# Reciprocal roots by one polynomial of degree 4, and low parts of twelve weight tiles by an adding DMA

## The chip, the cores and the metric

The kernel runs on one core of a Trainium2 chip. The time is that of the device for one execution, in microseconds, and a comparison of two kernels is one of medians on the same chip. TensorE (PE in the profile) multiplies matrices, VectorE (DVE), ScalarE (ACT) and GpSimd (POOL) work on tiles of 128 partitions, and SyncE (SP) issues DMAs. Each engine takes its own instructions in order, and semaphores make them wait for each other.

## What is computed

One step of a two-layer streaming encoder over 1,088 rows (1,024 of a new stream, 64 of a running one) of width 1,024, all in fp32. Layer 0 is a state-space mixer with a SwiGLU FFN, layer 1 a band attention with a SwiGLU FFN; each part stands between two root-mean-square norms.

```python
def rmsnorm(x, w):
    xf = x.astype(jnp.float32)
    y = xf * lax.rsqrt(jnp.mean(xf * xf, axis=-1, keepdims=True) + EPS)
    return (y * w.astype(jnp.float32)).astype(x.dtype)

def swiglu(u, w_in, w_out):
    g, up = jnp.split(u @ w_in, 2, axis=-1)
    return (jax.nn.silu(g) * up) @ w_out
...
        xp = xp + rmsnorm(mp, nw[1])
        xs = xs + rmsnorm(ms, nw[1])
        xp = xp + rmsnorm(swiglu(rmsnorm(xp, nw[2]), ffn_w_in[layer], ffn_w_out[layer]), nw[3])
        xs = xs + rmsnorm(swiglu(rmsnorm(xs, nw[2]), ffn_w_in[layer], ffn_w_out[layer]), nw[3])
```

`D_MODEL` is 1024 and the hidden width of the FFN 2816, so `w_in` is 1024 x 5632: 44 weight tiles of 128 columns, 22 for the gate and 22 for the other half.

## The kernel before

**Products of split numbers.** TensorE multiplies in a shortened format, fp32r. Each operand is split into a high part, its value rounded to fp32r, and a low part, the remainder; a product is three matmuls: high by high, high by low, low by high (lines 403 to 405, 1225 to 1227 and 1395 to 1397).

**Weight tiles.** The class `Weights` handles every weight tile in the order of use. `load` has SyncE fetch a tile of 128 x 1024 numbers, 512 KB, into one of two `raw` buffers (L220). `part` then writes the two parts into one slot of a ring: ScalarE copies the tile into fp32r, which gives the high part `h` (L300), and VectorE subtracts `h` from the tile, which gives the low part `lo` (L301). Some calls name GpSimd for the subtraction. After that the raw buffer is free for the next load, and SyncE, which takes its DMAs in order, waits in `load` until it is. The ring `hl` has three slots; while an FFN begins there are two more, `hx`.

**The start of an FFN.** `back` runs the last projection of the mixer or the attention (`project`), and while that runs, side tasks work on its results: `chain` applies the norm after the mixer, adds the residual, and applies the norm before the FFN for one quarter of the rows; `op_build` forms sums of blocks of the result and splits them into high and low parts (L1087, L1099, L1100). `ffn_plan` lists the weight tiles of the FFN: first ten single tiles, two for each of the first `NB0 = 5` hidden tiles, which `plain_pairs` multiplies in the plain way for the first 512 rows, then pairs of tiles for `run_pair`, which saves an eighth of the matmuls by sums of blocks. The ten single tiles are loaded and split while the projection and the norms still run.

**Reciprocal roots.** A norm sums squares: ScalarE squares a block (L425, L428) and GpSimd adds it to `ssum` (L429), through two buffers for squares. Then `rstd` has TensorE sum over partitions (`nst`, L436), and VectorE computes the reciprocal root on a column or so per block of 128 rows: mean plus epsilon (L442), a first guess from the bits of the number (L443), and two rounds of four instructions (L446 to L453), each a step of third order. `diag` puts the result on a diagonal (L457, tile `dg`), `bcast` spreads it over the partitions by a matmul with the constant matrix `frac` (tile `nbp`, L465), which carries a factor that the last round leaves out, and ScalarE copies that to `rb` (L469). `rstd` is called 40 times.

**Order.** The order of TensorE's instructions is written out: a main stream of matmul units, and side tasks that it starts when their time has come by its own count of microseconds, so an `nst` or `nbp` matmul stands at a fixed place among the units, and TensorE waits there if its input is late. The order on the other engines is set by a scheduler before the run, by priorities and expected times; `HIP`, `CHP` and `OPP` are such priorities. Steps of the roots have a high one.

Of the kernel before, what the change touches and what calls it, by code (L numbers as in the profile page):

```python
# [11 lines left out]
AF = mybir.ActivationFunctionType  # L12
ALU = mybir.AluOpType
# [20 lines left out]
FT = 22  # L34
# [26 lines left out]

PGS = (0,), (1,), (2,), (3,), (4,)
NB0 = 5
BIG = 1e30
MMR = 2360.0

C_NW = 0
# [129 lines left out]
class Weights:  # L197
# [95 lines left out]
    def part(self, it, key, ring, v, eng=None):  # L293
        if ring is not self.half:
            ring = self.hl if ring or self.hl.free() else self.hx
            self.used.append(ring)
        t, n = ring.get(), v.shape[1]
        h, lo = t[:, 0, :n], t[:, 1, :n]
        with self.tc.high_priority(self.pri):
            self.nc.scalar.copy(h, v)  # L300
            (eng or self.eng or self.nc.vector).tensor_tensor(lo, v, h, op=ALU.subtract)  # L301
        it[key] = h, lo
# [20 lines left out]
def hybrid_kernel(  # L323
# [5 lines left out]
    V, A, G, PE = nc.vector, nc.scalar, nc.gpsimd, nc.tensor  # L329
# [16 lines left out]
    ones = cp.tile([P, P], F32, name="ones")  # L346
    G.memset(ones, 1.0)
    frac = cp.tile([P, P], F32, name="frac")
    G.memset(frac, 9.0 / 64.0)
    pcs = cp.tile([P, NPC], F32, name="pcs")  # L350
    A.activation(ones[:, 0:1], ones[:, 0:1], AF.Square)

# [1 line left out]
    for _ in range(17):  # L354
# [13 lines left out]
    W = Weights(  # L368
        nc, Ring(wp, "raw", RAWB, [P, 1024]), Ring(wp, "hl", HLB, [P, 2, 1024], F32R),
        Ring(None, "half", 0, [P, 2, 512], F32R), Ring(None, "tt", 0, [P, 1024]),  # L370
    )
# [13 lines left out]
    def ax(name):  # L385
        return pax.tile([P, 512], F32, tag="ax", name=name)
# [8 lines left out]
    def passes(ps, w, rhs, ks, n, parts=2, first=True, last=True):  # L395
# [4 lines left out]
        for i, (kw, k) in enumerate(ks):  # L400
# [4 lines left out]
            PE.matmul(ps[:, :n], l_, xh, start=False, stop=(last and i == nk - 1))  # L405
            st.t += 3 * n / MMR
            if (i + 1) % cut == 0 and i + 1 < nk:
# [23 lines left out]
    def rstd(ssum, inv, r, nb, more=None):  # L431

        sp, ts = ax("nst"), [ssum] if more is None else [ssum, more]
        for i in range(nb):
            for j, t in enumerate(ts):
                PE.matmul(  # L436
                    sp[:, i:i + 1], t[:, i * P:(i + 1) * P], ones[:, 0:1], start=(j == 0), stop=(j == len(ts) - 1)
                )
        with tc.high_priority(HIP):
            v = nsb.tile([P, 12], F32, tag="nv", bufs=2, name="nv")  # L440
            a, h, y = v[:, 0:nb], v[:, 4:4 + nb], v[:, 8:8 + nb]
            V.tensor_scalar(a, sp[:, :nb], inv, EPS, op0=ALU.mult, op1=ALU.add)  # L442
            V.tensor_scalar(y.bitcast(I32), a.bitcast(I32), -0.5, float(0x5F3759DF), op0=ALU.mult, op1=ALU.add)  # L443

            for it in range(2):
                V.tensor_tensor(h, y, y, op=ALU.mult)  # L446
                if it:
                    V.scalar_tensor_tensor(a, h, 9.0 / 64.0, a, op0=ALU.mult, op1=ALU.mult)
                    V.scalar_tensor_tensor(h, a, -10.0 / 3.0, a, op0=ALU.add, op1=ALU.mult)
                else:  # L450
                    V.tensor_tensor(h, h, a, op=ALU.mult)
                    V.scalar_tensor_tensor(h, h, -10.0 / 3.0, h, op0=ALU.add, op1=ALU.mult)
                V.scalar_tensor_tensor(r if it else y, h, 5.0, y, op0=ALU.add, op1=ALU.mult)  # L453

    def diag(r3, nb):
        dg = DG.get()
# [15 lines left out]
    def rb_steps(ssum, n, out, wait=None, rb=None, more=None):  # L472

        nb = (n + P - 1) // P
        nr = nsb.tile([P, 4], F32, tag="nr", bufs=2, name="nr")
        rstd(ssum, 1.0 / D, nr[:, :nb], nb, more)
        yield 0.2, 0, DG.free
        with tc.high_priority(HIP):
            dg = diag(nr[:, :nb], nb)
        yield 0.1, wait or RB_WAIT  # L480
        with tc.high_priority(HIP):
            out.append(bcast(dg, 0, n, rb))
        yield 0.5, 0
# [107 lines left out]
    with ExitStack() as es:  # L591
# [8 lines left out]
        mask = sb1.tile([P, P], F32, name="mask")  # L600
        G.memset(mask, BIG)
        G.affine_select(mask, mask, pattern=[[1, P]], compare_op=ALU.is_ge, fill=-BIG, base=0, channel_multiplier=-1)
        stk = sb1.tile([64, 32], F32, name="stk")
# [167 lines left out]
        def ssd_task(j, s):  # L771
# [112 lines left out]
            if jj == 3:  # L884
                yield 0, 5.0
                rstd(ssg[:, s * 384:(s + 1) * 384], 1.0 / 512, rst[:, 3 * s:3 * s + 3, g], 3)
                rst_done.add((g, s))
                yield 0.3, 0
# [283 lines left out]

    def ffn_plan(layer):
        w1, w2 = w_f1[layer], w_f2[layer]
        W.plan(*[dict(src=[w1[i]]) for t_ in range(NB0) for i in (t_, FT + t_)])
        for t_ in [*range(NB0, FT), *range(NB0)]:
            W.plan(dict(src=[w1[t_], w1[FT + t_]]))
        for s in range(NSL):
            for m in range(KD):
                for k0, nk in KCH:  # L1180
                    W.plan(dict(src=[w2[m][:, k0 * P:(k0 + nk) * P]], n=nk * P))
# [27 lines left out]
    def run_pair(t_, pr, bs, ends, ops, hd, px, tmp, apart=False):  # L1209
# [3 lines left out]
        for (p_, key, c0, i), b in [(x, b) for b in bs for x in PRODS] if apart else [(x, b) for x in PRODS for b in bs]:  # L1213
# [9 lines left out]
            for k in range(4):  # L1223
# [4 lines left out]
                if k == 1:  # L1228
                    st.run(6 * n / MMR)
            st.t += 6 * n / MMR  # L1230
            if b in ends:
# [34 lines left out]
    def back(layer, start, cpost, xsrc, xmid, cpre, cpost2, xout, rb_out, done2):  # L1266
# [3 lines left out]
        with ExitStack() as es:  # L1270
# [79 lines left out]
            with ExitStack() as e2:  # L1350
# [18 lines left out]
                for r in ops[0].rings["a21"]:  # L1369
                    r.put()  # L1370
                for t_, bs, ends in [(t_, (0, 1), (0,) if t_ == FT - 1 else ()) for t_ in range(NB0, FT)] + [(t_, (1,), (1,) if t_ == NB0 - 1 else ()) for t_ in range(NB0)]:
                    run_pair(t_, W.get(), bs, ends, ops, hd, px, tmp, t_ == NB0)
                    W.pri = 0
# [7 lines left out]
            for s, (o, n) in enumerate(SL):  # L1381
# [3 lines left out]
                for m in range(KD):  # L1385
                    ps = px.tile([P, 512], F32, tag="mm", name="po")
                    for k0, nk in KCH:
                        w = W.get()
                        h, v = w["w"]
                        for k in range(k0, k0 + nk):  # L1390
# [7 lines left out]
                            if m == KD - 1:  # L1398
                                for c_ in c:
                                    cells.put(c_)  # L1400
                            st.run(3 * n / MMR)
                        W.put()
# [18 lines left out]
    def start_ssd(ops, px, after, dn):  # L1421
# [10 lines left out]
        st.spawn(op_build(ops[1], dn))  # L1432

    ffn_plan(0)
    rbp = pool(ctx, "rbp", side="right")
    rba = [rbp.tile([P, 384], F32, tag=f"rbf{s}", name="rbf") for s in range(NSL)]
# [4 lines left out]

    NEG = -BIG
    H2 = slice(0, 64), slice(64, 128)
# [7 lines left out]
    for b in range(2):  # L1451
        W.plan(*[dict(src=[w_o[m]]) for mg in MGS for m in mg])
    ffn_plan(1)
    done = done2
    uo = {}
# [403 lines left out]
```

## Time and profile before

| | |
|---|---|
| median of three runs | 3099.95 us (3099.75 to 3102.89) |
| the profiled execution | 3100.79 us, with a span of 3099.1 us in the trace |
| mean granted clock of TensorE | 0.988 |
| VectorE's subtractions in L301 | 407 instructions, of which 20 write `hx` |
| ScalarE's busy share | 45% |
| GpSimd's busy share | 28% |
| HBM over the span | 103 GB/s |

In the rows of a timeline the columns are: start, duration, engine, line, operation, the tile written and the tiles read, the shape, and how many were merged; in brackets the idle time of that engine before, and what ended it. Rows with a line of code and `x40` group instructions, with the shortest, median and longest duration in nanoseconds. A row of the windows gives a stretch of time and the busy time of each engine in it.

### The profile page before, as it was taken

How to read it: one execution, taken by the hardware profiler on the slowest of the kernel's cores; microseconds unless marked ns; L12 is line 12 of the kernel's file. 1: busy time of each engine (PE TensorE's matmuls, PEld its weight loads, DVE VectorE, ACT ScalarE, POOL GpSimd, SP SyncE). 2: the span in 40 equal slices, each digit the busy share in tenths (PEclk: the TensorE clock that was granted, in tenths of full speed). 3: DMA queues.
4: the chain of work that ended last, by engine and by line, in shares of the span. 5: the costliest groups of instructions: out<-in, count | busy, mean ns of one | idle time of the engine just before them, and what ended most of it. 6: DMA issues, size and time to landing. Idle time of an engine off the chain costs nothing.

```text
span 3099.1 us, 56834 instructions
## 1 busy us (share of the span) xinstructions
PE 2996.7 (97%) x21761; PEld 2913.0 (94%) x21761; DVE 2138.0 (69%) x4671; ACT 1407.2 (45%) x2500; POOL 875.6 (28%) x999
## 2 busy tenths in 40 slices
PE   8999999999999999999999999999998999999998
PEld 7899999999999999999999888889898999999997
DVE  7878788786778455584666888877778645575544
ACT  6656565664443222344443554444543322244432
POOL 2333333331334433441233111100053334342112
PEclk9999999999999999999999999999999999999999
DMA  3011111124534222245664121112344222245654
GB/s 118 32 59 48 59 51 59 49 79 150 167 119 122 78 74 80 90 146 169 201 193 127 61 68 61 54 60 61 122 137 142 80 77 75 79 123 177 207 183 131
DMA packets 174784, 322.85 MB, mean 104 GB/s; under 512 B 17168, under 2 KB 124560, under 8 KB 174512
## 3 DMA queue, kind: packets, MB, share of 16 engines
q1 hardware_dynamic: 174448, 319.16, 33.3%
q8 instruction: 171, 2.80, 0.4%
q14 instruction: 101, 0.83, 0.1%
q0 software_dynamic: 64, 0.07, 0.0%
HBM read 256.56 MB, written 62.60 MB: 103 GB/s over the span
## 4 chain that ended last, share of the span: by engine, by line
PE 77%; DVE 12%; DMA 4%; issue 3%; ACT 3%; POOL 2%; SPq 0%; DVEq 0%; POOLq 0%; ACTq 0%
PE mm L403 8%; PE px L1225 7%; PE px L1226 7%; PE px L1227 7%; PE mm L405 7%; PE mm L404 7%; PE po L1397 5%; PE po L1395 5%; PE po L1396 5%; PE mmx L403 2%; PE mmx L404 2%; PE mmx L405 2%; PE po L1651 2%; DVE hl L301 2%; PE ptp L1628 2%
## 5 line engine op out<-in xcount | busy, mean ns | idle before, releaser
L301 DVE TENSOR_TENSOR hl<-raw,hl 128x1024 fp32r<-128x1024 f32 (+1 forms) x299 | 369.5, 1237 | 316.0 <-ACT hl L300 315.7
L403 PE MATMUL mm<-r,hl 128*128 128x384 f32 (+2 forms) x1664 | 561.1, 337 | 7.4 <-ACT BT L737 5.9
L405 PE MATMUL mm<-r,hl 128*128 128x384 f32 (+2 forms) x1664 | 540.7, 325 | 0.6 <-DVE hl L301 0.6
L404 PE MATMUL mm<-r,hl 128*128 128x384 f32 (+2 forms) x1664 | 540.4, 325 | 0.0
L300 ACT CAST hl<-raw 128x1024 fp32r<-128x1024 f32 (+1 forms) x302 | 305.2, 1014 | 304.6 <-PE po L1397 96.5
L1226 PE MATMUL px<-r,hl 128*128 128x288 f32 (+1 forms) x1192 | 349.8, 293 | 0.0
L403 PEld LDWEIGHTS mm<-r,hl 128*128 128x128 f32 x1664 | 316.9, 190 | 16.6 <-issue 6.8
L429 POOL TENSOR_TENSOR ssum<-ssum,sq 128x256 f32<-128x256 f32 (+3 forms) x153 | 170.1, 1114 | 546.9 <-ACT sq L428 543.6
L1225 PE MATMUL px<-r,hl 128*128 128x288 f32 x1056 | 311.5, 295 | 6.5 <-DVE u L1240 6.5
L404 PEld LDWEIGHTS mm<-r,hl 128*128 128x128 f32 x1664 | 317.1, 191 | 0.6 <-DVE r L552 0.2
L405 PEld LDWEIGHTS mm<-r,hl 128*128 128x128 f32 x1664 | 316.2, 190 | 1.0 <-DVE hl L301 1.0
L1227 PE MATMUL px<-r,hl 128*128 128x288 f32 x1056 | 310.8, 294 | 0.0
L1227 PE MATMUL px<-rx,hl 128*128 128x256 f32 x816 | 228.9, 281 | 7.3 <-DVE hl L301 7.3
L1225 PE MATMUL px<-rx,hl 128*128 128x256 f32 x816 | 229.8, 282 | 0.0
L1226 PEld LDWEIGHTS px<-r,hl 128*128 128x128 f32 x1192 | 223.8, 188 | 0.1
L1396 PE MATMUL po<-rx,hl 128*128 128x384 f32 (+1 forms) x640 | 207.5, 324 | 0.0
L1225 PEld LDWEIGHTS px<-r,hl 128*128 128x128 f32 x1056 | 198.5, 188 | 8.2 <-DVE u L1240 8.2
L1395 PE MATMUL po<-rx,hl 128*128 128x384 f32 (+1 forms) x608 | 199.3, 328 | 0.0
L1397 PE MATMUL po<-rx,hl 128*128 128x384 f32 (+1 forms) x608 | 197.6, 325 | 0.9 <-DVE hl L301 0.9
L1227 PEld LDWEIGHTS px<-r,hl 128*128 128x128 f32 x1056 | 198.3, 188 | 0.0
L1226 PE MATMUL px<-rx,hl 128*128 128x256 f32 x680 | 190.7, 280 | 0.0
L258 POOL TENSOR_TENSOR tt<-raw 128x512 f32<-128x512 f32 x44 | 60.2, 1367 | 400.0 <-DMA raw<-in_w_f_dram 278.6
(343 smaller groups left out, 8135.5 us busy)
## 6 DMA issues: line engine op xcount, KB each, us to landing
raw<-in_w_f_dram SPq DMA_DIRECT2D x204, 512.0 KB, 3.7
raw<-in_w_in_dram SPq DMA_DIRECT2D x40, 512.0 KB, 3.6
raw<-in_w_f_dram SPq DMA_DIRECT2D x48, 384.0 KB, 3.2
sg<-hscr SPq DMA_DIRECT2D x88, 192.0 KB, 3.7
raw<-in_w_so_dram SPq DMA_DIRECT2D x32, 512.0 KB, 3.9
raw<-in_w_kv_dram SPq DMA_DIRECT2D x18, 512.0 KB, 3.6
raw<-in_w_o_dram SPq DMA_DIRECT2D x16, 512.0 KB, 3.8
sg<-hscr SPq DMA_DIRECT2D x44, 160.0 KB, 3.7
```

The lines of the kernel that those rows point to most:

```text
L300: self.nc.scalar.copy(h, v)
L301: (eng or self.eng or self.nc.vector).tensor_tensor(lo, v, h, op=ALU.subtract)
L403: PE.matmul(ps[:, :n], h_, xh, start=(first and i == 0), stop=False)
L404: PE.matmul(ps[:, :n], h_, xl, start=False, stop=False)
L405: PE.matmul(ps[:, :n], l_, xh, start=False, stop=(last and i == nk - 1))
L429: (eng or G).tensor_tensor(ssum[:, :n], ssum[:, :n], q[:, :n], op=ALU.add)
L1225: PE.matmul(ps, wh, ah[:, k, :], start=(k == 0), stop=False)
L1226: PE.matmul(ps, wh, al[:, k, :], start=False, stop=False)
L1227: PE.matmul(ps, wl, ah[:, k, :], start=False, stop=(k == 3))
L1395: PE.matmul(ps[:, :n], wh, xh, start=(k == 0), stop=False)
L1396: PE.matmul(ps[:, :n], wh, xl, start=False, stop=False)
L1397: PE.matmul(ps[:, :n], wl, xh, start=False, stop=(k == FT - 1))
```

## The change

It has two parts.

First, `rstd`. In place of two rounds of four instructions there is one polynomial: with y the first guess and h = a y y, a near 1, VectorE evaluates a polynomial of degree 4 in h by nested products and multiplies it by y. Two of the ten instructions of a root fall away. The leading factor of the polynomial is left out there and put into the constant matrix `frac`, as the factor before it was.

Second, `part`. For the first six single tiles of each FFN (`NACC = 3` hidden tiles, two tiles each) ScalarE writes the high part as before and then its negative into the slot of the low part. GpSimd issues a DMA that reads the tile from HBM once more and adds it to that: the low part. VectorE's subtraction for these twelve tiles falls away; the DMA stands in GpSimd's queue and waits there for the negation. The raw buffer is needed only for the copy.

```diff
@@ -61,7 +61,11 @@
 NB0 = 5
+
+NACC = 3
 BIG = 1e30
+
+RL, RP = 0.274060676, (-5.145514965, 10.804858208, -11.997578621, 8.987062454)
@@ -296,6 +300,14 @@
         h, lo = t[:, 0, :n], t[:, 1, :n]
+        if it.get("acc"):
+
+            with self.tc.high_priority(self.pri):
+                self.nc.scalar.copy(h, v)
+                self.nc.scalar.activation(lo, h, AF.Copy, scale=-1.0)
+            self.nc.gpsimd.dma_start(lo, it["src"][0], accum_op=ALU.add)
+            it[key] = h, lo
+            return
         with self.tc.high_priority(self.pri):
             self.nc.scalar.copy(h, v)
@@ -346,7 +358,7 @@
-    G.memset(frac, 9.0 / 64.0)
+    G.memset(frac, RL)
@@ -442,15 +454,13 @@
-            for it in range(2):
-                V.tensor_tensor(h, y, y, op=ALU.mult)
-                if it:
-                    V.scalar_tensor_tensor(a, h, 9.0 / 64.0, a, op0=ALU.mult, op1=ALU.mult)
-                    V.scalar_tensor_tensor(h, a, -10.0 / 3.0, a, op0=ALU.add, op1=ALU.mult)
-                else:
-                    V.tensor_tensor(h, h, a, op=ALU.mult)
-                    V.scalar_tensor_tensor(h, h, -10.0 / 3.0, h, op0=ALU.add, op1=ALU.mult)
-                V.scalar_tensor_tensor(r if it else y, h, 5.0, y, op0=ALU.add, op1=ALU.mult)
+
+            V.tensor_tensor(h, y, y, op=ALU.mult)
+            V.tensor_tensor(h, h, a, op=ALU.mult)
+            V.scalar_tensor_tensor(a, h, RP[0], h, op0=ALU.add, op1=ALU.mult)
+            V.scalar_tensor_tensor(a, a, RP[1], h, op0=ALU.add, op1=ALU.mult)
+            V.scalar_tensor_tensor(a, a, RP[2], h, op0=ALU.add, op1=ALU.mult)
+            V.scalar_tensor_tensor(r, a, RP[3], y, op0=ALU.add, op1=ALU.mult)
@@ -1172,7 +1182,7 @@
-        W.plan(*[dict(src=[w1[i]]) for t_ in range(NB0) for i in (t_, FT + t_)])
+        W.plan(*[dict(src=[w1[i]], acc=t_ < NACC) for t_ in range(NB0) for i in (t_, FT + t_)])
```

## The prediction

> **What bounds the kernel now.** I read the page first, then TensorE's timeline for its gaps, then the other engines' timelines around the largest of them.
>
> ```profile
> span 3099.1 us, 56834 instructions
> PE 2996.7 (97%) x21761; PEld 2913.0 (94%) x21761; DVE 2138.0 (69%) x4671; ACT 1407.2 (45%) x2500; POOL 875.6 (28%) x999
> L301 DVE TENSOR_TENSOR hl<-raw,hl 128x1024 fp32r<-128x1024 f32 (+1 forms) x299 | 369.5, 1237 | 316.0 <-ACT hl L300 315.7
> ```
>
> TensorE is busy for 97%, and the change removes none of its matmuls. Work taken from another engine pays only where TensorE waits for that engine: about 100 us in all. TensorE's waits at the start of the second layer's FFN, and others that stand behind a reciprocal root:
>
> ```profile
> 43.66 1.42 PE L465 MATMUL nbp<-dg,frac 128*128 128x384 f32 x4 [0.39 <-DVE dg L457]
> 969.49 0.58 PE L1227 MATMUL px<-rx,hl 128*128 128x256 f32 x1 [4.10 <-DVE hl L301]
> 1691.51 2.29 PE L436 MATMUL nst<-ones,ssum 128*128 128x1 f32 x10 [2.61 <-DVE ssum L1342]
> 2304.62 0.70 PE L465 MATMUL nbp<-dg,frac 128*128 128x256 f32 x2 [2.30 <-DVE dg L457]
> 2316.28 0.67 PE L465 MATMUL nbp<-dg,frac 128*128 128x256 f32 x2 [4.01 <-DVE dg L457]
> 2341.97 1.30 PE L465 MATMUL nbp<-dg,frac 128*128 128x288 f32 x2 [5.39 <-DVE nr L453]
> 2399.23 0.38 PE L1227 MATMUL px<-rx,hl 128*128 128x256 f32 x1 [3.18 <-DVE hl L301]
> ```
>
> Between 2296 and 2342 TensorE loses 2.30 + 4.01 + 5.39 = 11.7 us to three broadcasts of reciprocal roots. The windows say which engine is full there (columns: PE, PEld, DVE, ACT, POOL, granted clock, DMA share, GB/s):
>
> ```profile
> 2290.00:2310.00 20.00, 17.70 (x133) 17.18 (x132) 14.98 (x25) 10.76 (x26) 16.94 (x19) 1.00 0.56 173
> 2310.00:2330.00 20.00, 15.99 (x115) 15.73 (x114) 19.44 (x32) 13.18 (x22) 7.03 (x8) 0.91 0.37 123
> 2330.00:2350.00 20.00, 14.23 (x104) 13.52 (x102) 18.71 (x42) 7.80 (x13) 4.45 (x6) 0.91 0.29 89
> 885.00:915.00 30.00, 30.00 (x239) 29.89 (x238) 14.36 (x31) 10.72 (x17) 8.93 (x9) 1.00 0.41 136
> ```
>
> From 2310 to 2342 it is VectorE; before that, 2296 to 2310, GpSimd with 16.94 of 20. The last row is the same work in the first layer: VectorE half idle, TensorE full. The two FFN starts must be priced apart.
>
> **The low parts, second layer.** Six of VectorE's subtractions (L301) go; these are the six:
>
> ```profile
> 2301.94 1.76 DVE L301 TENSOR_TENSOR hl<-raw,hl 128x1024 fp32r<-128x1024 f32 x1
> 2306.60 1.23 DVE L301 TENSOR_TENSOR hl<-raw,hl 128x1024 fp32r<-128x1024 f32 x1 [2.03 <-ACT hl L300]
> 2310.52 0.80 DVE L1170 SCALAR_TENSOR_TENSOR rx<-rx,pcs,rb 128x256 f32<-128x256 f32 x1 [1.81 <-ACT rb L469]
> 2316.06 1.21 DVE L301 TENSOR_TENSOR hx<-raw,hx 128x1024 fp32r<-128x1024 f32 x1
> 2324.42 1.22 DVE L301 TENSOR_TENSOR hx<-raw,hx 128x1024 fp32r<-128x1024 f32 x1
> 2332.47 1.21 DVE L301 TENSOR_TENSOR hl<-raw,hl 128x1024 fp32r<-128x1024 f32 x1
> 2338.08 1.22 DVE L301 TENSOR_TENSOR hl<-raw,hl 128x1024 fp32r<-128x1024 f32 x1
> 2341.74 0.15 DVE L453 SCALAR_TENSOR_TENSOR nr<-nv 128x3 f32<-128x3 f32 x1
> ```
>
> From 2310.52, where VectorE gets the broadcast root, to 2341.74 it runs without a gap worth a microsecond, and the wait that ends at 2341.97 ends with it. Four of the six lie inside: 1.21 + 1.22 + 1.21 + 1.22 = 4.86 us. The first two lie before an idle of 1.81 us, so what they free is lost in that wait. Inside the stretch the shorter polynomial also drops 6 small instructions (2 from each of three roots), at 0.07 to 0.2 us of pitch as they lie interleaved: 0.4 to 1.2, taken as 0.6. Gain: **-5.5 us**, if the stretch starts when it did.
>
> It will not quite. What VectorE waited for at 2310.5 is a copy on ScalarE, which is queued behind squares that alternate with GpSimd's sums:
>
> ```profile
> 2297.60 1.05 ACT L300 CAST hl<-raw 128x1024 fp32r<-128x1024 f32 x1
> 2298.59 8.08 POOL L429 TENSOR_TENSOR ssum<-ssum,sq 128x256 f32<-128x256 f32 x9
> 2301.01 0.42 ACT L428 ACTIVATE sq<-rx 128x256 f32<-128x256 f32 x1 [0.40 <-DVE nv L446]
> 2305.53 1.03 ACT L300 CAST hl<-raw 128x1024 fp32r<-128x1024 f32 x1
> 2307.05 4.00 POOL L429 TENSOR_TENSOR ssum<-ssum,sq 128x288 f32<-128x288 f32 x4 [0.38 <-ACT sq L428]
> 2310.05 0.38 ACT L469 COPY rb<-nbp 128x256 f32<-128x256 f32 x1
> ```
>
> Two of the new negations fall here, behind the casts at 2297.60 and 2305.53. I price one like the cast, 1.05 us; ScalarE's gap between squares is 0.40, so each pushes the next square by 0.65. GpSimd, without a gap in 2298.6 to 2306.7, gets two DMA issues, and those wait in its in-order queue for the negations; behind them stand the sums, and for those wait the squares, the root's copy and TensorE. The trace has two DMAs issued by GpSimd, of 32 and 36 KB, both plain:
>
> ```profile
> L612 POOL DMA_DIRECT2D pbs<-in_pb_dram x1: 705/705/705, 2.5 to 2.5; - x1
> DMA to landing us min/median/max: 5.5/5.5/5.5
> L614 POOL DMA_DIRECT2D scs<-in_sconv_dram x1: 540/540/540, 3.2 to 3.2; - x1
> 869.27 2.29 POOL L429 TENSOR_TENSOR ssum<-ssum,sq 128x288 f32<-128x288 f32 x1 [5.58 <-ACT sq L428]
> raw<-in_w_f_dram SPq DMA_DIRECT2D x204, 512.0 KB, 3.7
> h<-in_h0T_dram SPq DMA_DIRECT2D x16, 64.0 KB, 1.9
> ```
>
> An issue costs GpSimd 0.54 to 0.71 there; a GpSimd sum beside a busy VectorE stretches to 2.29, and I use that as the upper price of an issue. Delay of the root's copy: 0 if both issues are scheduled behind the sums, 2 x 2.29 = 4.6 if both are in front and slow. I take 2 x (0.65 / 2 + 0.65) = **+2.0 us**, half of each push hidden under the issue, since these issues are the nearest rows. Net here -3.5.
>
> [...]
>
> **Does the data arrive in time?** From 64 to 512 KB the landing of a SyncE load grows by 1.8 us; 5.5 + 1.8 = 7.3 us for a GpSimd DMA, and 7.3 + 3.7 = 11 if the read of the destination adds a whole load. Tightest is the first tile of the first layer:
>
> ```profile
> 885.65 1.04 ACT L300 CAST hx<-raw 128x1024 fp32r<-128x1024 f32 x1
> 904.73 0.38 ACT L1197 ACTIVATE x<-mmx 128x256 f32<-128x256 f32 x1 [1.47 <-PE mmx L405]
> 2328.83 0.38 ACT L1197 ACTIVATE x<-mmx 128x256 f32<-128x256 f32 x1
> ```
>
> Cast and negation end at 887.7; the gate at 904.73 ends a unit of 24 matmuls, 3.0 us by the 239 in 30 us of the window above, so the tile is wanted at 901.7: 14 us for 7.3 to 11, hidden. Every microsecond over 14 would be a TensorE wait. In the second layer it is about 25 us, from 2299.7 to three before 2328.83. The raw buffer is also free one subtraction earlier, so SyncE's next weight load, and what is queued behind it, goes earlier; no wait above ends on it: nothing.
>
> **The low parts, first layer.** 885 to 915 holds all six; TensorE has no gap and VectorE is half idle. The subtractions there are worth nothing; six negations and issues fall on engines with two thirds idle: 0, with the GpSimd queue as a rival below.
>
> **The shorter polynomial.** Each root goes from 10 small VectorE instructions to 8. At the kernel's end they stand alone:
>
> ```profile
> 3083.54 0.16 DVE L442 TENSOR_SCALAR nv<-nst 128x3 f32<-128x3 f32 x1 [0.77 <-PE nst L436]
> 3085.50 0.56 DVE L457 TENSOR_TENSOR dg<-ident,nr 128x384 f32<-128x384 f32 x1
> 3086.11 1.43 PE L465 MATMUL nbp<-dg,frac 128*128 128x320 f32 x2 [2.62 <-DVE dg L457]
> ```
>
> Ten in 1.96 us: 0.196 each, 0.39 for a root. There are 40 roots, but the other 30-odd are under a busy TensorE. On the path: this one, the one that TensorE waits for at 43.66, and one in the chain before each of the waits at 969.49, 1691.51 and 2399.23. Five times 0.39: **-2.0 us** (bounds: -0.4, the tail alone, and -4, ten roots). The new constant in the broadcast matmul costs nothing.
>
> **The clock.** The two windows with 0.91 lose 0.09 x 20 = 1.8 us of clock each, one after the 4.01 wait and one after the 5.39; after the 2.30 there is none. At half rate TensorE does half of some 3.4 us: 1.7 lost. With 8.2 of 11.7 us of waiting left, I count half of one: **-0.9** (bounds 0 and -3.4). [...]
>
> **Sum:** -5.5 + 2.0 - 2.0 - 0.9 = -6.4. The profiled execution took 3100.8 (3099.1 of span and 1.7 around it), 0.8 above the median of the three runs; it goes to 3094.4, and the median 3099.95 to **3093.5**.
>
> **Rivals.**
>
> *More: the roots get ahead.* At 2316.28 the root's steps wait in VectorE's order between multiplications that need the late copy. With the subtraction at 2306.60 gone, the schedule may finish that root before them: then the 2.30 and 4.01 go, both dips too, and with half of the 5.39 left that is -9.0 - 3.4 - 2.0 + 2.0 = -12.4: 3087.5. Against it: VectorE is full until 2341 all the same.
>
> *Given back.* The delay of the copy comes out at its bound 4.6 and no dip goes: -5.5 + 4.6 - 2.0 = -2.9, 3097.0. For it: GpSimd has no gap there; the 2.30 saved before 2304 turns up again at 2316.
>
> *Slower: GpSimd's queue.* Its place is the stretch 2296 to 2313: an issue stands in front of the sums and waits for cast and negation (2.1), then takes 2.29: 4.4 us, for three tiles 13.2. In the first layer the same happens once ahead of sums that a root waits for. 13.2 + 4.4 - 5.5 - 2.0 = +10.1: 3110.0. It decides from (5.5 + 2.0) / 4 = 1.9 us for each of the four. For it: in-order queue and 16.94 of 20 busy; against it: the two issues shown took 0.6, and the schedule sets a DMA where its input is expected ready.
>
> *The adding DMA lands late*, beyond 14 us: at 20, +6.0 in the first layer, 3099.5; it needs twice the estimate.
>
> **How the numbers follow.** No change means within 0.2%, 3093.75 to 3106.15, about what a measurement of this kernel can tell. The forecast, with its own range 3090 to 3097, has 0.38 (0.25 faster, 0.13 same); more gain 0.15, faster; given back 0.20 and late landing 0.04, same; slower 0.23 (0.20 slower, 0.03 same). That makes 0.40, 0.40, 0.20. The range 3086 to 3109 takes in the first rival and most of the way to the third.
>
> **What would show it.** Right: in the changed profile GpSimd's 12 new issues at 0.5 to 1 us each; the three waits at 2304 to 2342 together under 9 us; VectorE 15 us (80 x 0.19) + 15 us (12 x 1.24) less busy; 8 instructions from mean square to diagonal in 1.6 us at the end. Wrong: GpSimd's issues, with their waits, above 1.9 us, the wait at 2316 longer than 6, a wait of TensorE on a weight tile's DMA, or new waits elsewhere because the order on VectorE or ScalarE has changed.

## The result, and the profile after

| | before | changed |
|---|---|---|
| median | 3101.42 us (4 runs, 3099.75 to 3104.03) | 3087.91 us (4 runs, 3083.24 to 3090.71) |
| the profiled execution | 3100.79, span 3099.1 | 3083.24, span 3081.1 |

The ratio is 0.9955, with a 95% interval of 0.9943 to 0.9967: 13.5 us less by the medians, where 6.4 were predicted. The sign is right and the time lies in the range (3086 to 3109), but outside the likeliest case's own range (3090 to 3097). The profiled execution of the changed kernel is the fastest of its four, so the 18.0 us between the two spans are more than the change is worth.

From the changed kernel's page, its span and the busy times:

```profile
span 3081.1 us, 56781 instructions
...
PE 2989.6 (97%) x21761; PEld 2908.2 (94%) x21761; DVE 2117.1 (69%) x4579; ACT 1419.9 (46%) x2512; POOL 880.4 (29%) x1011
```

VectorE is 20.9 us less busy, not the 30 that the prediction named. Line numbers are higher by 10 to 12 after the edit: L301 is L313, L429 is L441, L436 is L448, L465 is L475, L1170 is L1180, L1227 is L1237.

TensorE's timeline at the places whose rows the prediction quotes:

```profile
2285.55 0.50 PE L448 MATMUL nst<-ones,ssum 128*128 128x1 f32 x4
2292.54 0.70 PE L475 MATMUL nbp<-dg,frac 128*128 128x256 f32 x2
2296.88 1.01 PE L448 MATMUL nst<-ones,ssum 128*128 128x1 f32 x4 [3.64 <-POOL ssum L441]
2306.48 0.59 PE L475 MATMUL nbp<-dg,frac 128*128 128x256 f32 x2
2321.04 0.39 PE L416 MATMUL mmx<-r,hl 128*128 128x256 f32 x1 [1.37 <-DVE r L1110]
2327.78 0.72 PE L475 MATMUL nbp<-dg,frac 128*128 128x288 f32 x2 [1.64 <-DVE nv L461]
2384.03 0.39 PE L1237 MATMUL px<-rx,hl 128*128 128x256 f32 x1 [2.97 <-DVE hl L313]
```

The broadcasts that waited 2.30, 4.01 and 5.39 us before (now at 2292.54, 2306.48 and 2327.78) wait 0, 0 and 1.64. Two waits are new: 3.64 us for GpSimd's sums of squares, and 1.37 for a split sum of VectorE (before, 0.38). The losses fall from 12.1 us to 6.65.

The windows of that stretch (columns as before: PE, PEld, DVE, ACT, POOL, granted clock, DMA share, GB/s):

```profile
2280.00:2300.00 20.00, 16.34 (x111) 15.71 (x110) 14.49 (x24) 13.93 (x30) 16.25 (x21) 0.90 0.83 221
2300.00:2320.00 20.00, 19.67 (x146) 19.41 (x144) 17.29 (x28) 12.24 (x21) 9.91 (x11) 0.93 0.53 136
2320.00:2340.00 20.00, 17.32 (x139) 16.93 (x140) 19.86 (x42) 11.61 (x18) 7.81 (x10) 1.00 0.93 231
```

The clock is 0.90 and 0.93 in the first two, where it was 1.00 and 0.91: it dips at the new wait instead of the old ones. The dips themselves, two of before and then the one of the changed kernel:

```profile
2317.57:2320.98 3.41, 3.41 (x17) 3.41 (x16) 3.41 (x5) 1.17 (x4) 1.31 (x1) 0.50 0.78 243
2341.46:2344.87 3.41, 2.90 (x11) 2.65 (x12) 2.12 (x6) 0.40 (x1) 0.54 (x1) 0.50 0.22 88
2296.01:2302.83 6.82, 5.95 (x25) 5.95 (x26) 6.64 (x9) 3.64 (x7) 5.75 (x9) 0.50 1.01 261
```

The granted clock is 0.50 there, for 2 x 3.41 us before (the second time from 0.5 us ahead of the end of the wait of 5.39) and for 6.82 us at a stretch after. In this trace no dip is saved.

The adding DMA's line L308, with its issues (shortest, median and longest in ns, the first and the last start), what GpSimd was idle for ahead of them (us, times), and who waited for the data:

```profile
L308 POOL DMA_DIRECT2D hl<-in_w_f_dram x7: 862/877/889, 879.7 to 2327.5; - x7
L308 POOL DMA_DIRECT2D hx<-in_w_f_dram x5: 865/874/922, 877.5 to 2317.0; - x5
...
  ACT hx L307: 7.5, 3
  ACT hl L307: 7.4, 4
...
who waited for it (us, times):
...
DMA to landing us min/median/max: 5.7/7.9/10.4
```

An issue takes GpSimd 0.87 us, the data land after 5.7 to 10.4, and under the line for those who waited no matmul stands (what is left out there is a row of busy shares). The idle time of 14.9 us ahead of seven of the issues is GpSimd's wait for the negations.

To split the 18.0 us, two matmuls serve as marks: the nst of 2285.55 (2295.35 before) and the px of 2384.03 (2399.23). Ahead of the first the changed kernel gained 9.8 us, between them 5.4 (98.5 against 103.9), behind them 2.8. A second profile of the changed kernel (both_again below) is of an execution at its median, 3087.37; there it is 7.2, 3.9 and 2.8 of 13.8 us. In both, more than half was gained ahead of the first mark, and so ahead of any adding DMA of the second layer, whose first issue starts at 2292.27 and at 2294.55. That is what the experiments had to explain.

### The profile page after: what moved, and what is told of

It is laid out like the page before. It is cut to its first block, busy times and chain, and to the rows that moved or that the text cites. A ratio compares the mean times of both kernels' runs of the same rounds, so it can differ in the third digit from the quotient of the medians.

```text
span 3081.1 us, 56781 instructions
## 1 busy us (share of the span) xinstructions
PE 2989.6 (97%) x21761; PEld 2908.2 (94%) x21761; DVE 2117.1 (69%) x4579; ACT 1419.9 (46%) x2512; POOL 880.4 (29%) x1011
## 4 chain that ended last, share of the span: by engine, by line
PE 81%; DVE 10%; DMA 3%; issue 2%; ACT 2%; POOL 2%; SPq 0%; DVEq 0%; POOLq 0%; ACTq 0%
PE mm L415 8%; PE px L1235 8%; PE px L1236 8%; PE px L1237 8%; PE mm L417 8%; PE mm L416 8%; PE po L1407 5%; PE po L1405 5%; PE po L1406 5%; PE mmx L415 2%; PE mmx L416 2%; PE mmx L417 2%; PE po L1661 2%; PE ptp L1638 2%; DVE hl L313 1%
## 5 line engine op out<-in xcount | busy, mean ns | idle before, releaser
L313 DVE TENSOR_TENSOR hl<-raw,hl 128x1024 fp32r<-128x1024 f32 (+1 forms) x292 | 359.7, 1233 | 313.5 <-ACT hl L312 312.9
L312 ACT CAST hl<-raw 128x1024 fp32r<-128x1024 f32 (+1 forms) x295 | 297.8, 1014 | 302.1 <-PE po L1407 98.7
L441 POOL TENSOR_TENSOR ssum<-ssum,sq 128x256 f32<-128x256 f32 (+3 forms) x153 | 166.0, 1091 | 540.8 <-ACT sq L440 537.6
L1237 PE MATMUL px<-r,hl 128*128 128x288 f32 x1056 | 311.2, 295 | 0.0
L1237 PE MATMUL px<-rx,hl 128*128 128x256 f32 x816 | 229.1, 281 | 6.5 <-DVE hl L313 6.5
L1237 PEld LDWEIGHTS px<-r,hl 128*128 128x128 f32 x1056 | 198.4, 188 | 0.0
```

The source lines that it names most:

```text
L441: (eng or G).tensor_tensor(ssum[:, :n], ssum[:, :n], q[:, :n], op=ALU.add)
L1237: PE.matmul(ps, wl, ah[:, k, :], start=False, stop=(k == 3))
```

## The experiments

Each kernel was compared with runs of the kernel before on the same chip; the last column is the time between the two marks in each kernel's trace.

| kernel | median us | before, same chip | ratio (95%) | marks us |
|---|---|---|---|---|
| before | | | | 103.9 |
| poly_alone | 3093.97 | 3100.47 | 0.9976 (0.9966 to 0.9985) | 105.4 |
| dma_alone | 3093.86 | 3100.47 | 0.9977 (0.9967 to 0.9987) | 100.6 |
| poly_padded | 3100.38 | 3100.47 | 1.0001 (0.9992 to 1.0009) | 105.8 |
| both_again | 3087.37 | 3100.47 | 0.9955 (0.9942 to 0.9967) | 100.0 |
| no_dma | 3082.71 | 3098.90 | 0.9956 (0.9942 to 0.9970) | 95.9 |
| dma_layer2 | 3087.38 | 3098.90 | 0.9966 (0.9954 to 0.9977) | 100.0 |
| dma_ten | 3103.52 | 3098.90 | 1.0015 (1.0006 to 1.0023) | 115.4 |
| poly_short | 3088.01 | 3098.90 | 0.9970 (0.9959 to 0.9982) | 103.3 |
| dma_layer1 | 3094.04 | 3099.28 | 0.9984 (0.9975 to 0.9993) | 104.6 |
| degree3 | 3084.61 | 3099.28 | 0.9959 (0.9945 to 0.9972) | 99.4 |
| vector_sums | 3085.20 | 3099.28 | 0.9959 (0.9947 to 0.9971) | 97.0 |
| degree3_vector_sums | 3084.61 | 3099.28 | 0.9954 (0.9941 to 0.9968) | 95.6 |

The last column is of one trace each. The two traces of the changed kernel differ by 1.5 us there (98.5 and 100.0), so differences of that size say nothing. Part of it is the granted clock between the marks: 0.97 before, 0.90 to 0.93 in the four other kernels that subtract all of the second layer's tiles on VectorE, 0.95 to 0.98 in those that take six of them away, 0.88 in dma_ten.

### Each half alone

poly_alone:

```diff
-NACC = 3
+NACC = 0
```

> The polynomial without the adding DMA (all low parts by subtraction as before). Theory A, the prediction's own terms: five roots of 0.39 us and no dip saved, so 2.0 us less than before, ratio 0.9994. Theory B, from the lag between the two traces (TensorE already 12.5 us ahead at the end of the first layer's attention-free half, before any adding DMA of the second layer): the shorter root carries most of the gain, through about ten waits that each lose 0.4 us or more and through half-rate stretches of the clock that they no longer start; 7 to 11 us less, ratio 0.9965 to 0.9977. VectorE about 15 us less busy under both; the wait of 5.39 us on a broadcast at the second FFN start stays above 4 us under both.

dma_alone, which has the changed `part` and the old rounds in `rstd`:

```diff
-    G.memset(frac, RL)
+    G.memset(frac, 9.0 / 64.0)
...
-            V.tensor_tensor(h, h, a, op=ALU.mult)
-            V.scalar_tensor_tensor(a, h, RP[0], h, op0=ALU.add, op1=ALU.mult)
...
+            for it in range(2):
+                V.tensor_tensor(h, y, y, op=ALU.mult)
...
```

> The adding DMA with the two old rounds of the root. Theory A, the prediction's terms: -5.5 + 2.0 - 0.9 = 4.4 us less than before, all of it at the start of the second FFN, nothing in the first layer; ratio 0.9986. Theory B: the same 4 to 6 us at the second FFN start, and elsewhere lag against before stays within 1 us up to 2290 us. Rival C, that the two parts need each other (the gain at the second FFN start exists only if the roots there are also shorter): under 2 us, ratio above 0.9993.

both_again is the changed kernel, unedited.

> The changed kernel once more, beside its two halves on the same chip. 13.5 us less than before by the medians of the first comparison (ratio 0.9955, interval 0.9943 to 0.9967). If the parts add, the differences of the two halves sum to it within 2 us; if they share waits, the sum of the halves is larger.

Measured: 6.5 us for the polynomial, 6.6 for the adding DMA, 13.1 for both. The halves add, so rival C of dma_alone falls. For the polynomial theory A's 0.9994 lies outside the interval; theory B's range of ratios holds 0.9976, near its end. For the adding DMA 0.9986 is inside. The predicted wait at the FFN start can be read in both traces. TensorE's timeline of poly_alone:

```profile
2297.09 0.61 PE L448 MATMUL nst<-ones,ssum 128*128 128x1 f32 x4 [2.35 <-POOL ssum L441]
2307.23 1.19 PE L475 MATMUL nbp<-dg,frac 128*128 128x256 f32 x2 [3.07 <-DVE dg L467]
2335.61 1.30 PE L475 MATMUL nbp<-dg,frac 128*128 128x288 f32 x2 [4.17 <-DVE nr L463]
```

and of dma_alone:

```profile
2301.68 0.70 PE L475 MATMUL nbp<-dg,frac 128*128 128x256 f32 x2 [1.73 <-DVE dg L467]
2304.32 0.61 PE L448 MATMUL nst<-ones,ssum 128*128 128x1 f32 x4 [1.94 <-POOL ssum L441]
2312.95 0.67 PE L475 MATMUL nbp<-dg,frac 128*128 128x256 f32 x2
2328.41 0.39 PE L416 MATMUL mmx<-r,hl 128*128 128x256 f32 x1 [2.19 <-DVE r L1110]
2336.41 0.65 PE L475 MATMUL nbp<-dg,frac 128*128 128x288 f32 x2
```

The adding DMA is what ends the waits of 4.01 and 5.39: they are zero in dma_alone and still 3.07 and 4.17 in poly_alone. Over all traces they are 1.14 to 4.01 and 2.57 to 5.39 us in the kernels that subtract these tiles, and 0 to 0.96 and 0 to 1.64 in the others. The polynomial alone makes the first root earlier (the 2.30 goes) and meets GpSimd's sums instead (2.35). By the marks it gains nothing in this stretch. The windows between the marks, before and in poly_alone, show why (columns as above):

```profile
2295.35:2399.23 103.88, 87.92 (x684) 85.76 (x682) 88.17 (x164) 44.40 (x83) 45.09 (x49) 0.97 0.45 139
2287.19:2392.61 105.42, 91.55 (x684) 89.46 (x682) 86.62 (x152) 44.13 (x82) 44.97 (x48) 0.92 0.44 137
```

TensorE is idle for 13.9 us instead of 16.0, but its granted clock is 0.92 instead of 0.97. The 6.5 us come from elsewhere. They don't come from fewer half-rate stretches over the whole kernel, as theory B also had it: the mean granted clock is 0.987 over the 9 executions of poly_alone and over the 23 of before.

### Is the polynomial's gain its length?

poly_padded puts two further instructions of the same form into each root, which don't change its value:

```diff
             V.scalar_tensor_tensor(a, a, RP[2], h, op0=ALU.add, op1=ALU.mult)
+            V.scalar_tensor_tensor(a, a, 1.0, a, op0=ALU.mult, op1=ALU.max)
+            V.scalar_tensor_tensor(a, a, 1.0, a, op0=ALU.mult, op1=ALU.max)
```

> The polynomial alone with two more small VectorE instructions of the same form in each root (a value times one, maximum with itself), so ten instructions as before. If the gain of the polynomial is its length, all of it goes: within 1 us of before, ratio 0.9997 to 1.0003. If it comes from another order on VectorE or another clock pattern that any change of the program brings by chance, a difference of several us from before, of either sign, stays.

All of it goes: 1.0001. It is the length, together with the order that the scheduler gives VectorE for that length. The same run warns about traces: though its median is that of before, its wait at the second broadcast was 1.14 us where before shows 4.01, and its nst mark stands at 2296.75 instead of 2295.35. A wait of one trace may differ by 3 us without a difference in the time.

poly_short takes a further two away:

```diff
-RL, RP = 0.274060676, (-5.145514965, 10.804858208, -11.997578621, 8.987062454)
+RL, RP = 0.375, (-10.0 / 3.0, 0.0, 0.0, 5.0)
...
-            V.scalar_tensor_tensor(a, a, RP[1], h, op0=ALU.add, op1=ALU.mult)
-            V.scalar_tensor_tensor(a, a, RP[2], h, op0=ALU.add, op1=ALU.mult)
```

> The polynomial alone with two terms left out, of degree 2 (one step of third order), so six small instructions from the guess's square to the result become four and the roots are coarser; no adding DMA. Theory A, length alone: each two instructions of a root are worth what the padded kernel showed, 6.5 us, so 13 us less than before, 3087.5, ratio 0.9958. Rival B: many of the waits that the first two instructions shortened (0.39, 0.52, 0.35 us) are at zero by now, so the next two give about half, 3 us: 3091, ratio 0.9969. Rival C, five roots on the path: 2 us more, 3092.

10.9 us by the medians, ratio 0.9970, close to rival B's 0.9969. The second pair is worth 2 (by the ratios) to 4 us (by the medians) where the first was worth 6.5; its interval also holds the 0.9976 of poly_alone, so the time alone doesn't show that it is worth anything. Theory A's 0.9958 lies just outside the interval. Rival C can't be told from B by this run, but its five roots would have given the first pair 2 us, not 6.5.

Where the prediction had not looked: TensorE's timeline of before shows waits that don't name a root at all.

```profile
264.21 0.55 PE L785 MATMUL xtp<-ident,xsT 128*128 128x128 f32 x3 [0.52 <-ACT xsT L734]
...
862.40 0.40 PE L403 MATMUL mmx<-r,hl 128*128 128x288 f32 x1 [0.66 <-ACT r L551]
```

What a root has to do with the first of them shows on VectorE. The mixer's convolution (`cvt`, L730) feeds xsT, and it stands in VectorE's order behind a root of another norm. Before:

```profile
256.71 0.16 DVE L442 TENSOR_SCALAR nv<-nst 128x3 f32<-128x3 f32 x1 [1.35 <-PE nst L436]
...
259.42 0.17 DVE L453 SCALAR_TENSOR_TENSOR rst<-nv 128x3 f32<-128x3 f32 x1
259.50 0.48 DVE L813 TENSOR_TENSOR dm<-dm,CB 128x320 f32<-128x320 f32 x1
259.90 0.61 DVE L730 SCALAR_TENSOR_TENSOR cvt<-craw,pcs,cvt 128x384 f32<-128x384 f32 x1
```

and in poly_alone:

```profile
256.43 0.16 DVE L454 TENSOR_SCALAR nv<-nst 128x3 f32<-128x3 f32 x1 [1.22 <-PE nst L448]
...
258.62 0.15 DVE L463 SCALAR_TENSOR_TENSOR rst<-nv 128x3 f32<-128x3 f32 x1
258.69 0.48 DVE L823 TENSOR_TENSOR dm<-dm,CB 128x320 f32<-128x320 f32 x1
259.10 1.27 DVE L740 SCALAR_TENSOR_TENSOR cvt<-craw,pcs,cvt 128x384 f32<-128x384 f32 x2
```

From the root's first instruction to the convolution it is 3.19 us before and 2.67 after, 0.52 less, and TensorE's wait of 0.52 is gone (the same at 423 and at 582 us). TensorE has no wait that names this root; what waits is the work queued behind it.

Matmul by matmul, and leaving out the second FFN's start, there are nine places where every kernel with the shorter polynomial waits less than before, and dma_alone and poly_padded don't: at 43.7, 76.6 (5.95 to 4.82), 264, 423, 582, 697, 862, 969 and 3086 us of before. In poly_alone these are 0.35 to 1.13 us each and 4.9 us together; at 695 one wait of 0.65 is new. Not all of it is work behind a root. At 43.7, 697 and 3086 TensorE waits for a root itself. At 76.6 there is no root in VectorE's order between 44 and 77 us, neither before nor in poly_alone; there the scheduler has put the same instructions in another order. At 862 and 969 the cause was not followed. The nine places less the new wait make 4.2 us; for some 2 of the 6.5 us no place is shown.

### What the DMAs cost on GpSimd

no_dma leaves the addition out: the low parts of the twelve tiles stay negated high parts.

```diff
-            self.nc.gpsimd.dma_start(lo, it["src"][0], accum_op=ALU.add)
+            pass
```

> The changed kernel without the twelve adding DMAs: cast and negation stay, the low parts of these tiles stay negated high parts and the addition is left out. It prices what the DMAs cost on GpSimd. Theory A, the prediction's delay term in its measured size: two issues of 0.6 us of pitch and one wait for a square stand in front of the sums at the second FFN start, so the wait of 3.6 us on ssum there falls to about 2.1 and the time is 1 to 2 us under the changed kernel (3087.4), some 3085.5 to 3086.5, ratio to before 0.9949 to 0.9953. Rival B, that GpSimd's delay is hidden: within 0.7 us of the changed kernel. Rival C, that the second read of 6 MB also disturbs the loads or the engines: over 3 us under it, below 3084.

GpSimd's timeline of both_again, up to the sum that TensorE waits for:

```profile
2294.55 0.88 POOL L308 DMA_DIRECT2D hl<-in_w_f_dram  x1
2295.15 1.84 POOL L441 TENSOR_TENSOR ssum<-ssum,sq 128x256 f32<-128x256 f32 x2
2297.48 0.88 POOL L308 DMA_DIRECT2D hl<-in_w_f_dram  x1 [0.49 <-ACT sq L440]
2298.09 1.79 POOL L441 TENSOR_TENSOR ssum<-ssum,sq 128x256 f32<-128x256 f32 x2
```

The same wait of TensorE in both_again, and in no_dma:

```profile
2299.18 0.61 PE L448 MATMUL nst<-ones,ssum 128*128 128x1 f32 x4 [3.60 <-POOL ssum L441]
```

```profile
2301.88 0.61 PE L448 MATMUL nst<-ones,ssum 128*128 128x1 f32 x4 [1.55 <-POOL ssum L441]
```

Two issues stand in front of the last sums, and next to them a wait of 0.49 for a square, itself queued behind cast and negation. The wait falls by 2.05 us, the 2 of theory A, and between the marks 4.1 us go (2.6 against the first trace of the changed kernel). In the whole time the comparison doesn't decide: the median is 4.7 us under both_again's, in rival C's range, with a before that was 1.6 lower; the ratios are equal, and the interval holds all three theories. Rival B, hidden, is refuted at the place, not by the time.

### Which layer

```diff
-        W.plan(*[dict(src=[w1[i]], acc=t_ < NACC) for t_ in range(NB0) for i in (t_, FT + t_)])
+        W.plan(*[dict(src=[w1[i]], acc=layer == 1 and t_ < NACC) for t_ in range(NB0) for i in (t_, FT + t_)])
```

> The polynomial, and the adding DMA in the second layer's FFN alone; the first layer's six tiles are subtracted on VectorE as before. Prediction: the first layer's six are worth nothing, so the same as the changed kernel within 0.7 us, ratio to before 0.9953 to 0.9958. Rival: the 2 us by which the adding DMA alone gave more (6.6 by the medians) than the 4.6 that its trace shows between 2295 and 2345 us come from the first layer; then 2 us more than the changed kernel, about 3089.4, ratio 0.9964.

dma_layer1 has `layer == 0` instead.

> The polynomial, and the adding DMA in the first layer's FFN alone, the counterpart of the one in the second layer alone (whose ratio to before was 0.9966, interval 0.9954 to 0.9977, against 0.9955 for both). Prediction's term: six low parts of the first layer are worth 0, so the same as the polynomial alone, 6.5 us less than before, ratio 0.9974 to 0.9982. Rival: they are worth 2 us or more, ratio 0.9970 or less. The trace gives them at most 0.7 us: a wait of 0.77 us on ssum at 945 us that goes.

With the adding DMA in the second layer alone the median is both_again's, 3087.4, and the time between the marks is the same; the ratio, 0.9966, is nearer to the rival's 0.9964, but both theories are in its interval. dma_layer1 is plainer: 0.9984, beside 0.9976 for no adding DMA at all and a little above the predicted 0.9974 to 0.9982, and the rival's 0.9970 is outside. The first layer's six are worth nothing, as predicted.

### All ten tiles

```diff
-NACC = 3
+NACC = 5
```

> All ten single tiles of an FFN by the adding DMA instead of six. Theory A: at the second FFN start VectorE is no longer what the roots wait for (the waits of 4.01 and 5.39 us are at zero in the changed kernel), and the wait left is on GpSimd's sums, so four more subtractions taken from VectorE give under 1 us, and more issues in GpSimd's queue can take up to 2: 3086.5 to 3089.5, ratio 0.9952 to 0.9962. Rival B: VectorE still sets the wait of 2.47 us on a split sum (r, at 2323), and the four tiles remove it: 2 us less, below 3085.7, ratio under 0.9949.

Both theories missed: 3103.5, slower than before. ScalarE's, GpSimd's and TensorE's timelines of dma_ten:

```profile
2364.48 1.04 ACT L306 CAST hl<-raw 128x1024 fp32r<-128x1024 f32 x1
```

```profile
2366.91 0.87 POOL L308 DMA_DIRECT2D hl<-in_w_f_dram  x1 [1.32 <-ACT hl L307]
2368.92 0.85 POOL L308 DMA_DIRECT2D hl<-in_w_f_dram  x1 [1.15 <-ACT x L1207]
```

```profile
2376.32 0.58 PE L417 MATMUL mmx<-rx,hl 128*128 128x256 f32 x1 [10.26 <-DMA hl<-in_w_f_dram]
```

Of L308 in the whole of dma_ten, who waited (us, times), and of the tile hl around these two issues, the landing:

```profile
  PE mmx L417: 19.0, 4
```

```profile
DMA to landing us min/median/max: 9.4/9.9/10.4
```

In this kernel the later tiles are split only when a slot of the ring is free again, shortly ahead of their use. From the first cast to the matmul it is 11.8 us, of which the landing of the first DMA takes 9.4 (2366.91 to 2376.3); in both_again the same pair's casts begin at 2359.96, and after one subtraction TensorE goes on at 2362.31, 2.35 later. That wait of 10.26 us and three more, two of them in the first layer, make 19.0 us, where the median is 16.1 above both_again's. The rival "lands late" of the prediction is real; with six tiles the data are early, with ten they aren't.

### Two attempts at a better version

degree3 has one term less, with other coefficients:

```diff
-RL, RP = 0.274060676, (-5.145514965, 10.804858208, -11.997578621, 8.987062454)
+RL, RP = -0.31307308, (-4.20188974, 7.00085189, -6.99310217)
...
-            V.scalar_tensor_tensor(a, a, RP[2], h, op0=ALU.add, op1=ALU.mult)
-            V.scalar_tensor_tensor(r, a, RP[3], y, op0=ALU.add, op1=ALU.mult)
+            V.scalar_tensor_tensor(r, a, RP[2], y, op0=ALU.add, op1=ALU.mult)
```

> The changed kernel with a polynomial of degree 3 in place of 4, seven small instructions in a root instead of eight, with a largest error of 7.5e-7 of the root by its fit. By the two steps of the length measured so far (two instructions fewer gave 6.5 us, four gave 10 to 11) one more is worth about 2 us: 3085, ratio 0.9948. Rival: what is left of the roots' waits is at other engines, under 0.5 us.

vector_sums:

```diff
-                add_sq(s2, ym, n, m == 0)
+                add_sq(s2, ym, n, m == 0, V if layer and q == 1 and m > 4 else None)
```

> The changed kernel with the last three of the seven sums of squares of the second quarter of rows, before the second FFN, on VectorE instead of GpSimd. In the changed kernel TensorE waits 3.6 us for these sums, which stand on GpSimd between two DMA issues, and VectorE is idle for 3.70 us just then. Theory: three sums of 0.9 us and one issue leave the chain for three of about 0.45, so the wait falls to 1.5 us or less: 2 us less than the changed kernel, ratio 0.9948. Rival: what follows (VectorE without a gap from 2312 to 2330) takes it back, under 0.7 us; or the sums stand in VectorE's order behind a subtraction of 1.75 us and nothing is gained.

degree3_vector_sums has both edits.

> Both of these together: the changed kernel with degree 3 and with three sums of the second quarter on VectorE. If they add, 4 us less than the changed kernel, 3083, ratio 0.9942; if the stretch after it takes the sums' gain back, like degree 3 alone, 0.9948.

The medians are 2 to 3 us under both_again's, against a before that was 1.2 lower; the ratios, 0.9954 to 0.9959, can't be told from 0.9955, nor from the 0.9948 that degree3 and vector_sums were expected to reach. At its place vector_sums did what it was to do, as its trace shows:

```profile
2297.55 0.58 PE L448 MATMUL nst<-ones,ssum 128*128 128x1 f32 x4 [0.79 <-DVE ssum L441]
2305.54 0.67 PE L475 MATMUL nbp<-dg,frac 128*128 128x256 f32 x2 [0.96 <-DVE dg L467]
2321.76 0.39 PE L416 MATMUL mmx<-r,hl 128*128 128x256 f32 x1 [2.95 <-DVE r L1110]
```

The wait falls from 3.60 to 0.79. Of these 2.8 us about 1.0 comes back at the second broadcast, which waited for nothing in both_again, and 0.5 at the split sum; between the marks 3.0 us are gained against both_again, and 1.5 against the other trace of the changed kernel. Whether that is also gained in the time stays open.

## Why the prediction was half right

**The second FFN's start was sized well, by the wrong course.** Predicted were -5.5 + 2.0 - 0.9 = -4.4. Between the marks the adding DMA gives -3.3 beside the old roots (103.9 to 100.6) and -5.4 beside the new ones (105.4 to 100.0), each from single traces. The prediction had the 5.39 shrink and the copy come 2 us later. In fact the broadcasts' waits went nearly whole, as in the rival "the roots get ahead", and the loss moved to GpSimd's sums and to a split sum: the new waits that the prediction named as a sign of being wrong. So the agreement is partly luck. The rival's number, 3087.5, is the measured one, by luck too: it left the new waits out, counted both dips of the clock as gone, and kept the -2.0 for the polynomial.

**The delay by GpSimd had about the right size, at another place.** It appears at the nst and not at the copy. Predicted were +2.0, of which 1.3 for the two issues and the rest for the negations. In no_dma, which keeps the negations, the wait is 2.05 shorter, so that is the price of the issues alone. Against poly_alone, which has neither (2.35), the 3.60 of both_again is 1.25 more. An issue was priced 0.65 and took 0.87, but the sum behind it starts 0.6 after it. The rival "GpSimd's queue" decides from 1.9 us an issue and is far off: no issue here took over 0.93 us.

**The clock term is not shown.** -0.9 for half a dip. No run shows that term. What the trace of before shows is 3.41 us at a granted clock of 0.50 behind the wait of 4.01, with the same matmul ahead of the wait and in the dip:

```profile
2309.58 0.29 PE L405 MATMUL mmx<-r,hl 128*128 128x288 f32 x1
2309.71 0.29 PE L403 MATMUL mmx<-r,hl 128*128 128x288 f32 x1
...
2318.54 0.45 PE L404 MATMUL mmx<-r,hx 128*128 128x288 f32 x1
2318.78 0.45 PE L405 MATMUL mmx<-r,hx 128*128 128x288 f32 x1
```

It starts every 0.13 us ahead of it and every 0.24 in it, so the dip costs an estimated 3.41 x 0.11 / 0.24 = 1.6 us, where the prediction had 1.7. In the changed kernel's first trace the dips only moved with the waits: 0.90 and 0.93 stand where 1.00 and 0.91 stood, the clock is at 0.50 for 6.82 us in both, and between the marks it is 0.97 in both; in both_again it is 0.95. But the one trace of before has the best clock of the five kernels that subtract there (0.90 to 0.97), so a single pair of traces can't say what the adding DMA saves of it.

**The first layer, the landing and the earlier loads were right.** Zero, 7.3 to 11 us estimated against 5.7 to 10.4, and no wait on a weight tile's DMA.

**The polynomial was mis-sized, and this is the step that failed.** The prediction said that of 40 roots "the other 30-odd are under a busy TensorE" and priced five at 0.39. Measured: 6.5 us, with -2.0 outside the interval (4.7 to 10.5 us by the ratios). The price of one root was right, since at the end the eight instructions from mean square to diagonal take 1.6 us and the wait is 2.23 instead of 2.62. The count was wrong. Of its five places three shrank in poly_alone, by 0.39, 0.61 and 0.39; at 1691.51 it was 0.2 in some kernels and nothing in others, and at 2399.23 poly_padded waits as little. What it left out were the waits that don't name a root's tile, though the work that they wait for stands behind a root in VectorE's order (264, 423 and 582 us, 1.6 us together), one at 697 that does name a root (0.35), one at 862 that wasn't followed (0.47), and the order that the scheduler chooses (1.1 at 76.6).

**VectorE's busy time.** 30 us less was named as a sign; it is 20.9, or 10.7 by the polynomial alone (80 instructions of 0.13, not 0.19) and 6.8 by the adding DMA alone, where 12 x 1.24 should have gone. Part of that is given back, as told below.

What stays open: 6.6 us by the medians for the adding DMA alone, of which its marks show 3.3. Its interval (4.0 to 10.2 us) holds the predicted 4.4. Against poly_padded, which runs as long as before, the marks show 5.2 (105.8 to 100.6), so the rest may lie in the one trace of before. The mean granted clock is 0.988 over the executions of dma_alone and 0.987 over those of before; whether that is an effect of the change isn't shown.

## What to carry to other kernels

A short chain on an in-order engine also delays what is queued behind it, not only those who wait for its result (0.52 us at 264): to price a shorter chain, go through all waits of the bounding engine, whatever tile they name, and look in the order of the shortened engine for what stands ahead of it. To hand a subtraction to an adding DMA traded here 1.24 us of VectorE for 7.9 us (the median) from issue to landing, so it paid for data prepared long ahead, and turned into a wait of 10.26 us where a buffer came free just before use. Where two engines race for the same stage, taking work from the one that ends last moves the wait to the next (here from VectorE's 4.01 and 5.39 to 3.64 on GpSimd's sums); the gain is the difference. It is read between fixed marks of the bounding engine rather than from one wait, with the granted clock beside it and from more than one trace.

## What the runs showed of the hardware

In four traces (both_again, the changed kernel's first, dma_alone, dma_layer2) a single instruction of VectorE that runs beside an issue of GpSimd's, with sums right behind it, takes 2.43, 2.22, 2.41 and 2.41 us and ends within 0.3 us of the end of these sums. VectorE's timeline of both_again:

```profile
2302.07 2.43 DVE L1180 SCALAR_TENSOR_TENSOR rx<-rx,pcs,rb 128x256 f32<-128x256 f32 x1
2304.41 0.15 DVE L455 TENSOR_SCALAR nv<-nv 128x2 int32<-128x2 int32 x1
2304.49 0.47 DVE L1180 SCALAR_TENSOR_TENSOR rx<-rx,pcs,rb 128x256 f32<-128x256 f32 x1
```

and GpSimd's:

```profile
2301.73 0.88 POOL L308 DMA_DIRECT2D hx<-in_w_f_dram  x1
2302.32 1.88 POOL L441 TENSOR_TENSOR ssum<-ssum,sq 128x288 f32<-128x288 f32 x2
```

The multiplication begins 0.34 us after the issue and lasts 2.43 us, to 2304.50, 0.3 after the sums; the same form takes 0.47 once GpSimd is idle. In the changed kernel's first trace it is the small step L455 that meets the issue:

```profile
2300.10 2.22 DVE L455 TENSOR_SCALAR nv<-nv 128x2 int32<-128x2 int32 x1
```

2.22 us in place of 0.15, to 2302.32, again to the end of GpSimd's second sum (2302.28). Not every one does: in the same trace the diagonal (L467) of 2291.63 ends at 2292.49, 0.2 into the issue of 2292.27. In no_dma, with sums but no issue beside them, single ones of these multiplications take at most 1.10. So one instruction of VectorE takes some 2 us more here (2.43 for 0.47, 2.22 for 0.15), where the issue delays GpSimd's next sum by 0.6. That is a part of what is missing in VectorE's busy time; how much of the 4.1 us that no_dma wins between the marks comes of it is not shown, since 2.05 of them are the wait at the nst and 0.64 the wait at the split sum (2.47 to 1.83). It isn't settled whether it is the issue or the sums behind it that make these instructions longer.

One more row of both_again points to the sums:

```profile
2298.48 1.69 DVE L1180 SCALAR_TENSOR_TENSOR rx<-rx,pcs,rb 128x256 f32<-128x256 f32 x1 [3.70 <-ACT rb L479]
```

This multiplication starts after the issue of 2297.48 has ended (2298.36), and it ends 0.3 us after the sums of 2298.09 (2299.88).
